# GDN's first half projected from an operand without its norm's factor, gate tiles moved within GDN's order, and the FFN's first tiles kept and interleaved

## The chip, the cores and the metric

The kernel runs on one core of a Trainium2 chip, as one program. The metric is the time of one execution on the device, in microseconds. It is the median of three runs. TensorE is PE below, VectorE is DVE, ScalarE is ACT, GpSimd is POOL; SyncE (SP) issues the transfers (DMAs). Every engine works through its own instructions in program order.

## The reference

It is one inference step of a small decoder trunk: two layers, each a token mixer and a SwiGLU feed forward, on one new sequence of 512 tokens and eight decoding sequences of 4 tokens, 544 tokens of 1024 features in all. The weights are shared.

```python
for i in range(DEPTH):                       # DEPTH = 2
    hn = rms_norm(x, mix_pre_norm[i])
    if i % N_MIXERS == 0:
        out, S, cbuf = gdn_mixer(hn, ...)    # gated DeltaNet
    else:
        out, hs, cbuf = ssd_mixer(hn, ...)   # Mamba-2 SSD
    x = x + rms_norm(out, mix_post_norm[i])
    hn = rms_norm(x, ffn_pre_norm[i])
    f = (silu(hn @ ffn_w_gate[i]) * (hn @ ffn_w_up[i])) @ ffn_w_down[i]
    x = x + rms_norm(f, ffn_post_norm[i])

def rms_norm(x, w):  return x * rsqrt(mean(x * x) + 1e-6) * w

def gdn_mixer(h, ...):                       # 8 heads of 128
    qkv, z, b, a = split(h @ w_in)           # 24 + 8 tiles of 128 columns, and b, a
    q, k, v = split(silu(causal_conv(qkv)))  # 4 taps; then q and k are l2-normed
    beta, g = sigmoid(b), -exp(A_log) * softplus(a + dt_bias)
    o, S = gated_delta_chunked(q, k, v, g, beta, S0)   # a triangular solve per chunk, then a scan
    o = rms_norm(o, norm_w) * silu(z)
    return o @ w_out, S, conv_new
```

Everything is fp32. The outputs are x of all tokens and the new states of both mixers.

## The kernel before, in words

**Layout.** Features lie on the partitions, tokens along the free axis. The 544 tokens are two halves of H2 = 272; half 1 ends with the 32 decoding tokens. Each weight tile of 128 output columns is multiplied with half 0 and with half 1; one such product of a tile with a half is called a *unit*. A unit over 1024 features (8 slices of 128) has 24 matmuls, since an fp32 product is made of three: each operand is split into a high part and a remainder, and `product` (L235) issues wh·xh, wh·xl and wl·xh for each slice (L240 to L242). The b and a columns go through `narrow` (L249).

**Weights.** `fetch_to` loads weights in pieces of 4 slices (256 KB) on SP's queue, AHEAD = 4 pieces ahead of the unit that uses them, into 4 raw buffers. `split` makes wh on ACT (L212) and wl on DVE (L213). A tile whose two units don't follow each other is loaded and split twice.

**Stages.** GDN (b and a, called ba, and 32 tiles k, q, v, z of the eight heads, then wo, its output projection of 8 tiles), FFN0 (22 pairs of a gate tile g and an up tile u, then 8 down tiles of 22 slices, 66 matmuls per unit), SSD (in the same manner; its wo has 16 slices, 48 matmuls per unit) and FFN1.

**Order.** `Flow` carries an estimated clock. Each unit advances it by `flow.product`; the rest of the work (conv, scan, norms) is written as generators, tasks that say with each `yield` after how many estimated microseconds the next step is put into the program. So the delays, constants in the code, set where a step stands among the matmuls of each engine's program; nothing is ordered at run time.

- `start_first(tiles, op, lead)` (L1146) puts `lead` tiles of half 0 first, the same tiles of half 1 next, and takes the rest tile by tile, both halves. GDN has lead 1 (ba alone), FFN0 and FFN1 lead 10 (g and u of five pairs, NL = 5).
- `ab(tiles, op, tail)` (L453) is for the projections at a stage's end: tile by tile, and for the last `tail` tiles all units of half 0 first and then those of half 1. So half 0 is whole `tail` units before the stage ends, and its norm and update run under half 1's units. Tails are 4 in GDN's wo, 3 in the FFN's down and 3 in SSD's wo.

**Norms.** `Squares` squares each feature slice on ACT (L368) and sums on DVE (L375). `rsq` reduces over the partitions with a small matmul (ms, L347), and makes the inverse root of it in a dozen small DVE steps (L319 on). `spread` brings it to all partitions (dg on DVE, L336, then a matmul r, L339). `Pre` is the norm ahead of a stage: with `free=False` each slice is multiplied with the factor (xn, L411) and split into xh and xl, the operand; with `free=True` the operand is made of x times the norm's weight alone (xh L309, xl L310), before the factor is known, and the factor is multiplied to the products. Ahead of both FFNs it is free. `Post` is the norm behind a stage: its `finish` multiplies the projected slices with the factor (fw, L446), adds them to x (L448, every third on POOL) and squares the new x for the next `Pre`.

**GDN's end.** Each head's scan ends with products into `sc` (L978 to L996). A pair's output is normed by `o_norm` (oss L1058, os L1065, then dg, r, a multiply by the weight and factor, L1088, and by silu(z), og, L1091) and split into oh and ol, wo's operand.

Before the first unit, both halves are squared, normed and split, and the flow is drained.

## Time and profile before

| | |
|---|---|
| time, median of 3 runs | 1762.46 us (1761.85 to 1764.05) |
| time of the profiled execution | 1758.35 us |
| its span | 1756.6 us |
| busy: PE, DVE, ACT, POOL | 1680.5, 1165.7, 820.1, 113.0 us |
| mean granted clock of PE | 0.985 |
| GDN with wo | 0 to about 424.6 us |
| FFN0 | to about 849 us |
| SSD with wo | to about 1322 us |
| FFN1 | to 1756.6 us |

Busy time is the time in which an engine executes; matmuls are pipelined, so a busy PE is not yet a PE at full pace. The ends of the stages are read from the first matmul with the next stage's operand. A wait in the profile is the idle time of an engine in front of an instruction, with the instruction that released it.

### The profile page before, as it was taken

Reading aid. Unit: us, or ns where it says so; the run is one execution under the profiler, and the core shown is the slowest. Engines: PE = TensorE matmul, PEld = TensorE weight load, DVE = VectorE, ACT = ScalarE, POOL = GpSimd, SP = SyncE. Lnnn points to the kernel's source line nnn. Section 1 sums busy time; section 2 is a strip of 40 time slices with the busy share of each in tenths; the row PEclk is TensorE's granted clock in tenths of the full one; section 3 lists DMA queues with packets and bytes.
Section 4 is the critical chain, followed back from the end, with each engine's and each line's share of the span. In section 5 each row is a group of like instructions: output and inputs, shape, how many; then the busy total and the mean of one; then the engine's idle time right before and its main releaser. Section 6 shows DMA issues by size and latency. Waiting matters only on the chain. (4 is left out here: it accounts for less than half of the span.)

```text
span 1756.6 us, 37084 instructions
## 1 busy us (share of the span) xinstructions
PE 1680.5 (96%) x14127; PEld 1599.9 (91%) x14127; DVE 1165.7 (66%) x3077; ACT 820.1 (47%) x1830; POOL 113.0 (6%) x335
## 2 busy tenths in 40 slices
PE   4999999998999999999699999999999999999997
PEld 4988888998899999999587899999998999999996
DVE  7895866457876655326878787878358766565346
ACT  4665554445543333325465565657355533333242
POOL 1122112000000000000001110100000000000000
PEclk9999999998999999999899999999999999999998
DMA  5332333343554423225534544432444644444444
GB/s 149 112 90 81 88 91 94 100 140 108 155 176 144 144 98 91 78 82 159 182 110 129 166 142 141 132 105 68 148 134 139 202 141 139 145 141 131 133 142 129
DMA packets 164275, 222.97 MB, mean 127 GB/s; under 512 B 53312, under 2 KB 66176, under 8 KB 163584
## 3 DMA queue, kind: packets, MB, share of 16 engines
q1 hardware_dynamic: 164096, 220.59, 41.5%
q8 instruction: 111, 1.82, 0.4%
q14 instruction: 68, 0.56, 0.1%
HBM read 199.49 MB, written 21.04 MB: 126 GB/s over the span
## 5 line engine op out<-in xcount | busy, mean ns | idle before, releaser
L242 PE MATMUL mm<-xh,wl 128*128 128x272 f32 x2560 | 747.9, 293 | 9.5 <-DVE wl L213 9.1
L240 PE MATMUL mm<-xh,wh 128*128 128x272 f32 x2560 | 752.9, 294 | 0.9 <-ACT raw L533 0.9
L241 PE MATMUL mm<-xl,wh 128*128 128x272 f32 x2560 | 747.2, 292 | 0.0
L212 ACT ACTIVATE wh<-wr 128x512 fp32r<-128x512 f32 (+1 forms) x564 | 349.3, 622 | 415.5 <-PE mm L241 372.3
L213 DVE TENSOR_TENSOR wl<-wr,wh 128x512 fp32r<-128x512 f32 (+1 forms) x564 | 380.3, 678 | 242.0 <-ACT wh L212 230.1
L240 PEld LDWEIGHTS mm<-xh,wh 128*128 128x128 f32 x2560 | 485.6, 190 | 15.6 <-issue 8.6
L242 PEld LDWEIGHTS mm<-xh,wl 128*128 128x128 f32 x2560 | 483.8, 189 | 16.1 <-DVE wl L213 12.2
L241 PEld LDWEIGHTS mm<-xl,wh 128*128 128x128 f32 x2560 | 485.6, 190 | 6.7 <-issue 3.3
L240 PE MATMUL mm<-gb,wh 128*128 128x272 f32 x544 | 157.6, 291 | 0.0
L242 PE MATMUL mm<-gb,wl 128*128 128x272 f32 x544 | 155.3, 288 | 0.0
L241 PE MATMUL mm<-gb,wh 128*128 128x272 f32 x544 | 155.0, 288 | 0.0
L546 DVE SCALAR_TENSOR_TENSOR conv<-raw,cw,conv 128x512 f32<-128x512 f32 x144 | 106.9, 742 | 14.7 <-ACT conv L543 14.0
L240 PEld LDWEIGHTS mm<-gb,wh 128*128 128x128 f32 x544 | 102.2, 188 | 1.3 <-ACT wh L212 0.3
L241 PEld LDWEIGHTS mm<-gb,wh 128*128 128x128 f32 x544 | 102.2, 189 | 0.4
L242 PEld LDWEIGHTS mm<-gb,wl 128*128 128x128 f32 x544 | 101.6, 188 | 0.3
L448 POOL TENSOR_TENSOR x<-x,fw 128x272 f32<-128x272 f32 x16 | 16.1, 1004 | 1069.7 <-DVE fw L446 545.2
L1171 ACT ACTIVATE sg<-sg 128x272 f32<-128x272 f32 x88 | 37.9, 431 | 95.1 <-DVE sg L1170 94.7
L375 DVE TENSOR_TENSOR acc<-acc,sq 128x272 f32<-128x272 f32 x112 | 51.0, 459 | 44.6 <-ACT sq L368 43.9
L241 PE MATMUL mm<-yl,wh 128*128 128x272 f32 x256 | 74.3, 291 | 1.2 <-DVE yl L310 1.2
L242 PE MATMUL mm<-yh,wl 128*128 128x272 f32 x256 | 73.7, 290 | 0.8 <-DVE wl L213 0.8
L240 PE MATMUL mm<-yh,wh 128*128 128x272 f32 x256 | 74.0, 289 | 0.0
L1179 DVE TENSOR_TENSOR sg<-sg,mm 128x272 f32<-128x272 f32 x88 | 38.4, 436 | 50.6 <-PE mm L242 50.3
(398 smaller groups left out, 2456.5 us busy)
## 6 DMA issues: line engine op xcount, KB each, us to landing
wr<-f_d_in SPq DMA_DIRECT2D x110, 256.0 KB
wr<-f_g_in SPq DMA_DIRECT2D x108, 256.0 KB
wr<-f_u_in SPq DMA_DIRECT2D x108, 256.0 KB
wr<-g_w_in SPq DMA_DIRECT2D x64, 256.0 KB
wr<-s_w_in SPq DMA_DIRECT2D x48, 256.0 KB
wr<-s_wo_in SPq DMA_DIRECT2D x44, 256.0 KB
wr<-s_wz_in SPq DMA_DIRECT2D x36, 256.0 KB
ar<-ad SPq DMA_DIRECT2D x32, 272.0 KB
```

The source lines that it names most:

```text
L212: S.activation(out=hi, in_=src, func=AF.Copy)
L213: V.tensor_tensor(out=lo, in0=src, in1=hi.bitcast(F32), op=ALU.subtract)
L240: PE.matmul(ps, lhsT=h[:, k, :], rhs=ah(k0 + k), start=first and k == 0, stop=False)
L241: PE.matmul(ps, lhsT=h[:, k, :], rhs=al(k0 + k), start=False, stop=False)
L242: PE.matmul(ps, lhsT=lo[:, k, :], rhs=ah(k0 + k), start=False, stop=last and k == n - 1)
L375: V.tensor_tensor(out=self.acc, in0=self.acc, in1=self.late, op=ALU.add)
L448: E.tensor_tensor(out=x[:, k, :], in0=x[:, k, :], in1=f, op=ALU.add)
L546: V.scalar_tensor_tensor(out=Y[:, 0:SEQ], in0=R[:, j:j + SEQ], scalar=w[:, j:j + 1], in1=Y[:, 0:SEQ], op0=ALU.mult, op1=ALU.add)
L1171: S.activation(out=t, in_=t, func=AF.Silu)
L1179: V.tensor_tensor(out=t, in0=t, in1=ps, op=ALU.mult)
```

## The change

It has three parts and a number of changed constants.

1. **The first half of GDN without the factor.** `Pre` of half 0 is now free, that of half 1 not (`FREE_G`). Products of half 0 that come before the factor are held in PSUM (`st.held`) and finished when it is there; from then on `scaled` multiplies each product of half 0 with the factor, on DVE, in place of ACT's copy. Both halves' norms are tasks of the flow. Three tiles of half 0 (ba, k0, k1) come first, then the same of half 1 (`GLEAD` = 3). At the head of SP's queue ba's weights and the constants are moved between the halves of x, and the small loads and the zeros are moved behind.
2. **Three gate tiles moved forward.** z0, z1 and z2 stand among the k, q and v tiles; z3 to z7 stay at the end.
3. **Four kept tiles.** g0, u0, g1 and u1 of FFN0 are loaded and split during GDN's wo into buffers of their own (kh, kl). FFN0 starts with them on half 0, then g2.0 g2.1 u2.0 u2.1 … u4.1, then g0.1 u0.1 g1.1 u1.1, then the rest tile by tile (the number behind the dot is the half).

Beside that: the tails are 5 in GDN's wo, 4 in the down projections and 4 in SSD's wo; the delays of the tasks are named constants, some with other values; a sixth buffer for squares, which dg now shares.

```diff
-NSQ = 5
+NSQ = 6
+KEPT = 4
+HELD = 3
-NEWTON = 3.0
+ORDER = ("k0 k1 z0 q0 q1 z1 k2 k3 v0 v1 z2 q2 q3 k4 k5 v2 v3 q4 q5 k6 k7 v4 v5 q6 q7 v6 v7 "
+         "z3 z4 z5 z6 z7")
+GLEAD = 3
+FREE_G = (True, False)
+NEWTON = 2.5
+T_G = 5
+T_F = 4
+T_S = 4
...
@@ emit
+        if len(st.held[0] + st.held[1]) >= (HELD if wide else 2):
+            flow.until(lambda: st.r[hf] is not None)
...
-        done(hf, ps)
+        if st.free[hf] and st.r[hf] is None:
+            st.held[hf].append((done, ps))
+        else:
+            done(hf, ps)
...
@@ Pre.end
+            if self.free:
+                st.ready[self.hf] = True
+                yield 0.0, FACTOR
...
+                while st.held[self.hf]:
+                    done, ps = st.held[self.hf].pop(0)
+                    done(self.hf, ps)
...
+    def scaled(out, ps, hf):
+        if st.free[hf]:
+            V.tensor_tensor(out=out, in0=ps, in1=st.r[hf][0:ps.shape[0]], op=ALU.mult)
+        else:
+            V.tensor_copy(out=out, in_=ps)
...
@@ Conv.done, half 0
+                    if st.free[0]:
+                        scaled(R[:, 3:3 + H2], ps, 0)
+                        ps = R[:, 3:3 + H2]
...
-        order = ("k0 k1 q0 q1 k2 k3 v0 v1 q2 q3 k4 k5 v2 v3 q4 q5 k6 k7 v4 v5 q6 q7 v6 v7 "
-                 "z0 z1 z2 z3 z4 z5 z6 z7").split()
+        order = ORDER.split()
...
-        for u in units(start_first(tiles, xop, 1)):
+        us = units(start_first(tiles, xop, GLEAD))
...
@@ GDN's wo
-        for u in units(ab(tiles, op, tail=4)):
+        todo = [(i, s) for i in range(KEPT) for s in pieces([io["f_u" if i % 2 else "f_g"][0, i // 2]])]
+        us = units(ab(tiles, op, tail=T_G))
+        for n, u in enumerate(us):
             emit(u, True, True)
+            for _ in range(2 - n % 2):
+                if todo:
+                    i, s = todo.pop(0)
+                    kept[i].append(keep(wk, s))
...
@@ ffn
-        for u in units(start_first(tiles, xop, 2 * NL)):
+        if kept is None:
+            us = units(start_first(tiles, xop, 2 * NL))
+        else:
+            first = [[(srcs, hf, xop, done) for srcs, done in tiles[:KEPT]] for hf in range(2)]
+            rest = [(srcs, hf, xop, done) for srcs, done in tiles[KEPT:] for hf in range(2)]
+            n = 2 * (2 * NL - KEPT)
+            us = units(first[0] + rest[:n] + first[1] + rest[n:],
+                       {id(tiles[i][0]): kept[i] for i in range(KEPT)})
```

**The head of SP's queue.** nrm are the norms' weights, cst the constants, wr<-g_ba_in the weights of ba, cw and hist the conv's weights and history, xd<-kqm the zeros. Before:

```order
L103 DMA cst<-cst_in 128x816
L103 DMA nrm<-nrm_in 128x64
L103 DMA x<-xT_in 128x2x272 x8
L103 DMA cw<-g_cw_in 128x96
L103 DMA hist<-g_hist_in 128x576
...
L103 DMA xd_281<-kqm 128x16x16 x2
L103 DMA xd_282<-kqm 128x16x16 x2
L103 DMA wr<-g_ba_in 128x256 x2
L103 DMA wr<-g_w_in 128x512 x2
```

And after:

```order
L133 DMA nrm<-nrm_in 128x64
L133 DMA x<-xT_in 128x2x272 x4
L133 DMA wr<-g_ba_in 128x256
L133 DMA cst<-cst_in 128x816
L133 DMA x<-xT_in 128x2x272 x4
L133 DMA wr<-g_w_in 128x512 x3
L133 DMA cw<-g_cw_in 128x96
L133 DMA hist<-g_hist_in 128x576
...
L133 DMA xd_110<-kqm 128x16x16 x2
```

The weights moved ahead of the small loads and the zeros, and half 1's x behind ba's weights and the constants.

**PE at the end of GDN.** sc are a head's scan products, oss and os the sums of o_norm, mm the wide matmuls: with xh, xl of a z tile, with oh, ol of wo. Before, the last pair's rows stand between matmuls of the z tiles:

```order
L996 MATMUL sc<-E,w 128x128
...
L1058 MATMUL oss<-osq,cst 32x272 x2
...
L1058 MATMUL oss<-osq,cst 32x272 x2
...
L1065 MATMUL os<-cst,oar 68x4 x4
...
L240 MATMUL mm<-oh,wh 128x272
...
L339 MATMUL r<-dg,cst 128x272
```

After:

```order
L1062 MATMUL sc<-w,kp 128x128
L1133 MATMUL oss<-osq,cst 32x272 x2
L279 MATMUL mm<-oh,wh 128x272
L1070 MATMUL sc<-qT,S 128x128
L1071 MATMUL sc<-E,w 128x128
...
L1133 MATMUL oss<-osq,cst 32x272 x2
...
L1140 MATMUL os<-cst,oar 68x4 x4
...
L388 MATMUL r<-dg,cst 128x272 x4
```

The last scan product, the second oss and os moved behind wo's first matmuls; the four spreads r stand together, 37 wide matmuls behind os.

**PE from wo into FFN0.** ms and r are the sum and the spread of a norm; the two xh are the operands of the two halves, kh and kl a kept tile. Before, from half 0's spread on, with half 1's first product at the end:

```order
L339 MATMUL r_6169<-dg_6167,cst_80 128x272
...
L240 MATMUL mm_6405<-xh_6172,wh_6408 128x272
L241 MATMUL mm_6405<-xl_6173,wh_6408 128x272
L347 MATMUL ms_6300<-cst_80,acc_5710 68x1 x4
...
L339 MATMUL r_6369<-dg_6367,cst_80 128x272
...
L240 MATMUL mm_6895<-xh_6372,wh_6824 128x272
```

After:

```order
L388 MATMUL r_6209<-dg_6207,cst_80 128x272
...
L281 MATMUL mm_6350<-oh_5615,wl_6305 128x272
L279 MATMUL mm_6403<-xh_6212,kh_5708 128x272
...
L396 MATMUL ms_6453<-cst_80,acc_5743 68x1 x4
...
L388 MATMUL r_6524<-dg_6522,cst_80 128x272
...
L279 MATMUL mm_6616<-xh_6212,wh_6406 128x272
...
L279 MATMUL mm_6686<-xh_6527,wh_6406 128x272
```

Half 0's spread stands further ahead of FFN0's first matmul, that one uses a kept tile, half 1's sum and spread stand further behind it, and half 1's first product is five units behind, where it was ten.

More of the change, by code (lines that the diff above doesn't have):

```diff
@@ L38 @@
 RAWW = 3 + SEQ + NB * 7
+ORDER = ("k0 k1 z0 q0 q1 z1 k2 k3 v0 v1 z2 q2 q3 k4 k5 v2 v3 q4 q5 k6 k7 v4 v5 q6 q7 v6 v7 "
+         "z3 z4 z5 z6 z7")
+GLEAD = 3
+FREE_G = (True, False)
+FREE_S = (False, False)
+NEWTON = 2.5
+TILE = 1.0
+FACTOR = 5.0
+D_FIN = 2.5
+D_DEC0 = 8.0
+D_DEC1 = 3.5
+D_DEC = 3.5
+D_KT = 3.5
+D_QT = 11.0
+D_VT = 2.5
+D_ON = 3.0
+D_XT = 6.0
+D_WT = 16.0
+D_GT = 2.0
+D_INV = 1.0
+D_MG = 3.0
+D_S1 = 0.8
+D_S2 = 1.2
+D_X3 = 3.0
+D_BT = 1.5
+D_B0 = 0.0
+T_G = 5
+T_F = 4
+T_S = 4
 BIG = 1.0e30
@@ L180, in _program @@
     st.turn = 0
+    st.free = [False, False]
+    st.held = [[], []]
     def half(i):
@@ L233, in fetch_to, with keep, product @@
             ready.append((h, lo))
-    def product(ps, wi, ah, al, first=True, last=True, k0=0):
-        h, lo = ready[wi]
+    def keep(where, src):
+        r = wraw.tile([P, src.shape[1], P], F32, tag="w", name="wr")
+        dma(r, src)
+        h = where.tile([P, src.shape[1], P], F32R, tag="h", name="kh")
+        lo = where.tile([P, src.shape[1], P], F32R, tag="l", name="kl")
+        split(h, lo, r)
+        return h, lo
+    def product(ps, w, ah, al, first=True, last=True, k0=0):
+        h, lo = w
         n = h.shape[1]
@@ L265, in pieces, with units @@
         return out
-    def units(seq):
+    def units(seq, kept={}):
         out, held = [], None
         for srcs, *rest in seq:
+            if id(srcs) in kept:
+                out.append((srcs, *rest, len(plan), kept[id(srcs)]))
+                held = None
+                continue
             if held != id(srcs):
@@ L463, in ab @@
         return seq
-    pres = [Pre(hf, 0, 0) for hf in range(2)]
-    for pre in pres:
-        for k in range(KD):
-            pre.square(k)
-    for pre in pres:
-        flow.start(pre.end())
-    flow.drain()
     from_dram = [io["xT"][:, :, half(0)], io["xT"][:, :, half(1)]]
@@ L638, in ba_done @@
         def ba_done(hf, ps):
-            V.tensor_copy(out=ba[:, half(hf)], in_=ps[0:64])
+            scaled(ba[:, half(hf)], ps[0:64], hf)
             if hf == 0:
@@ L666, in ba_done @@
             rows(gd, Gc)
-            flow.start(decay(0), 8.0)
+            flow.start(decay(0), D_DEC0)
             S.activation(out=neG, in_=Gc, func=AF.Exp)
@@ L704, in k_after @@
                 pr[p].inv = 0
-            flow.start(k_task(h), 4.5)
+            flow.start(k_task(h), D_KT)
         def k_task(h):
@@ L753, in k_task @@
             if pr[p].inv == 2:
-                flow.start(invert(p), 1.0)
+                flow.start(invert(p), D_INV)
         def invert(p):
@@ L807, in invert @@
                 dma(xd[1][p][:, r, r], XT[32 * s:32 * s + 32])
-            flow.start(merge(p), 2.0)
+            flow.start(merge(p), D_MG)
         def merge(p):
@@ L928, in v_after @@
             S.activation(out=v, in_=Y, func=AF.Silu)
-            flow.start(v_task(h, v), 2.5)
+            flow.start(v_task(h, v), D_VT)
         def v_task(h, v):
@@ L965, in ended @@
                 if hasattr(hd[h ^ 1], "ended"):
-                    flow.start(o_norm(p), 3.0)
+                    flow.start(o_norm(p), D_ON)
         def scan(h):
@@ L1112, in gdn, with first @@
             names[id(tiles[-1][0])] = n
-        for u in units(start_first(tiles, xop, 1)):
-            n = names.get(id(u[0]))
-            if n is not None and u[1] == 0 and n[0] == "k":
+        us = units(start_first(tiles, xop, GLEAD))
+        fetch_to(1)
+        dma(cst, io["cst"])
+        load_x(1, 2)
+        fetch_to(3)
+        def first(hf):
+            pre = Pre(hf, 0, 0, FREE_G[hf])
+            for k in range(KD):
+                pre.square(k)
+                yield 0.0, 0.0 if hf == 0 else D_BT
+            yield from pre.end()
+        flow.start(first(0))
+        flow.start(first(1), D_B0)
+        for i, u in enumerate(us):
+            flow.until(lambda: st.ready[u[1]])
+            n = names.get(id(u[0]))
+            if i == 1:
+                load_small()
+            if i == 2 * GLEAD - 1:
+                if GLEAD > 2:
+                    flow.start(decay(1), D_DEC1)
+                load_zeros()
+                og += [act.tile([P, 4, T], F32, tag="x", name="og") for _ in range(2)]
+            if n is not None and u[1] == 0 and i >= GLEAD and n[0] == "k":
                 h = int(n[1])
@@ L1153, in start_first, with ffn @@
         return seq
-    def ffn(layer, last, before, lx, items):
+    def ffn(layer, last, before, lx, items, kept=None):
         fx = ExitStack()
@@ L1225, in ffn @@
             tiles.append(([w], post.tile(m)))
-        for u in units(ab(tiles, op, tail=3)):
+        for u in units(ab(tiles, op, tail=T_F)):
             emit(u, True, True)
@@ L1286, in dt_done @@
             dtT = dt_done.t
-            V.tensor_copy(out=dtT[:, half(hf)], in_=ps[0:64])
+            scaled(dtT[:, half(hf)], ps[0:64], hf)
             if hf == 0:
@@ L1523, in f @@
                     sz[m] = t544("sz")
-                S.activation(out=sz[m][:, half(hf)], in_=ps, func=AF.Silu)
+                t = sz[m][:, half(hf)]
+                if st.free[hf]:
+                    scaled(t, ps, hf)
+                    ps = t
+                S.activation(out=t, in_=ps, func=AF.Silu)
                 if hf:
-                    flow.start(gate(m), 2.0)
+                    flow.start(gate(m), D_GT)
             return f
@@ L1599, in ssd @@
         tiles = [([io["s_wo"][m]], post.tile(m)) for m in range(8)]
-        for u in units(ab(tiles, op, tail=3)):
+        for u in units(ab(tiles, op, tail=T_S)):
             emit(u, True, True)
```

119 lines of the change are left out of this document (70 added, 49 removed).

## The prediction

> **What bounds the kernel.** First the page's busy times, then the chain that ended last, then the waits of PE (us in total, times, longest), to see which engine carries the span and where it stands still.
>
> ```profile
> PE 1680.5 (96%) x14127; PEld 1599.9 (91%) x14127; DVE 1165.7 (66%) x3077; ACT 820.1 (47%) x1830; POOL 113.0 (6%) x335
> PE 23%; DVE 2%; ACT 0%; issue 0%; DVEq 0%; ACTq 0%
> PE ms L347 <- DVE acc L375: 28.2, 6, 11.1
> PE r L339 <- DVE dg L336: 13.6, 5, 6.4
> PE mm L242 <- DVE wl L213: 9.9, 10, 3.1
> ```
>
> PE bounds it: busy 96%, and the chain is PE nearly everywhere. The change takes no matmul away, so it can win only where PE stands still or runs slowly, and the waits say where that is: at the norms (ms waits for the squares' sum, r for the spread factor) and, less, for split weights. The waits name lines, not places, so I cut the span into windows at the seams of the stages (us, busy time and count of PE, PEld, DVE, ACT, POOL, then granted clock, DMA share, GB/s).
>
> ```profile
> 0.00:34.58 34.58, 11.19 (x57) 8.53 (x57) 24.26 (x77) 17.01 (x41) 4.26 (x20) 1.00 0.63 155
> 75.00:125.00 50.00, 48.57 (x646) 43.53 (x644) 46.73 (x171) 31.32 (x83) 12.69 (x42) 1.00 0.41 105
> 314.00:372.30 58.30, 58.30 (x470) 54.86 (x471) 25.97 (x68) 22.61 (x60) 0.66 (x4) 1.00 0.29 90
> 372.30:424.60 52.30, 52.15 (x405) 51.12 (x404) 34.69 (x83) 30.97 (x73) 1.03 (x1) 1.00 0.48 149
> 424.60:475.00 50.40, 41.30 (x295) 39.12 (x294) 44.98 (x128) 28.59 (x62) 3.61 (x3) 0.90 0.41 126
> 475.00:665.00 190.00, 190.00 (x1495) 189.30 (x1494) 124.39 (x275) 69.36 (x133) 0.00 (x0) 1.00 0.44 141
> 832.00:876.00 44.00, 29.31 (x216) 26.57 (x214) 37.91 (x112) 22.60 (x49) 4.34 (x12) 0.87 0.59 190
> 1322.00:1372.00 50.00, 46.65 (x344) 44.90 (x343) 44.76 (x125) 29.00 (x61) 1.75 (x2) 0.93 0.50 154
> ```
>
> The row 475 to 665 is FFN0 in full flow: 1495 matmuls in 190 us, 0.127 us each, nothing idle. A window's loss is its length less 0.127 us for each matmul in it: 12.9 us on the way into FFN0 (424.6 to 475), 16.6 from FFN0 into SSD (832 to 876), 6.3 from SSD into FFN1 (1322 to 1372); wo (372.3 to 424.6) loses 0.9. In the head 57 short matmuls are done in 34.58 us, a loss of about 27. These four places are what the change can reach. In the GDN's interior DVE, 46.7 of 50 us, is nearly as full as PE.
>
> **A, the head: −4 us (bounds −9 and 0).** Columns: start, length, engine, instruction, wait before it in brackets.
>
> ```profile
> 9.76 2.77 ACT L368 ACTIVATE sq<-x 128x272 f32<-128x272 f32 x7
> 10.26 4.73 SPq L103 DMA_DIRECT2D xd<-kqm  x4
> 17.23 1.27 PE L339 MATMUL r<-dg,cst 68*128 68x272 f32 x2 [1.25 <-DVE dg L336]
> 24.95 1.28 PE L339 MATMUL r<-dg,cst 68*128 68x272 f32 x2 [6.44 <-DVE dg L336]
> 25.73 2.31 PE L249 MATMUL mm<-xh,whl 128*64 128x272 f32 x8
> 32.77 0.79 DVE L213 TENSOR_TENSOR xl<-xn,xh 128x272 fp32r<-128x272 f32 x2
> 32.95 1.16 PE L249 MATMUL mm<-xl,whl 128*64 128x272 f32 x8
> 34.58 0.39 PE L240 MATMUL mm<-xh,wh 128*128 128x272 f32 x1
> ```
>
> Before, both halves are squared, normed and split before the first wide matmul at 34.58, half 1's r at 24.95 after a wait of 6.44, and its last xl ends at 33.56. ba and k0, k1 of both halves come after that; four wide units of 24 matmuls, 24 × 0.127 = 3.05 us each, make 12.2, so k1 is done at 34.6 + 12.2 = 46.8. After the change half 0's operand needs no factor: squares and splits run as x lands, and I estimate it complete at 12 us (eight squares and eight copies on ACT, some 0.4 us each, from 5.5 us on). The ba weights are issued before the constants, and the four DMAs of zeros (4.73 us of SP's queue at 10.26) come behind. So ba, k0 and k1 of half 0, two wide units and the narrow ones, are done by about 22, and lie under the making of half 1's operand. Half 1's x now lands behind ba's weights and the constants, so I put its operand 2 us later, at 35.5; with the 1 us of ba behind it, as before, and half 1's own two wide units, 6.1, k1 is done at 42.6. Gain 46.8 − 42.6 = 4. At best half 1, for which ACT and DVE are free sooner, is 3 us earlier than before (−9); at worst its chain slips by the whole gain, since ACT and DVE now also split the first weights there (0). The first x8 of ba takes 2.31 us where the x8 at 32.95 takes 1.16, so PE's start is at half speed; that too now lies under the wait. Half 0's three products are held in PSUM until the factor is there, which nothing on PE waits for before half 1.
>
> **B, the price of the free half: 0 us (−3 to +5).** 33 products of half 0 (24 conv tiles, 8 gates, ba) go through a DVE multiply in place of an ACT copy.
>
> ```profile
> 0.73 1.28 ACT L365 ACT_TABLE_LOAD   x1 [0.73 <-PEq L1695]
> L1179 DVE TENSOR_TENSOR sg<-sg,mm 128x272 f32<-128x272 f32 x88 | 38.4, 436 | 50.6 <-PE mm L242 50.3
> 349.43 0.39 PE L996 MATMUL sc<-E,w 128*128 128x128 f32 x2
> 368.73 0.60 PE L1065 MATMUL os<-cst,oar 128*68 128x4 f32 x8
> 369.37 0.17 DVE L319 TENSOR_SCALAR nx<-os 68x16 f32<-68x16 f32 x1 [2.61 <-PE os L1065]
> 382.70 0.79 DVE L213 TENSOR_TENSOR ol<-og,oh 128x272 fp32r<-128x272 f32 x2 [0.56 <-ACT oh L212]
> L336 DVE TENSOR_TENSOR dg<-cst,ny 68x272 f32<-68x272 f32 x20 | 8.7, 434 | 0.3
> L1091 DVE TENSOR_TENSOR og<-og,qT 128x544 f32<-128x544 f32 x8 | 5.8, 720 | 0.0
> ```
>
> A like multiply out of PSUM takes 436 ns (L1179), so 33 × 0.436 = 14.4 us of DVE over some 330 us, of which eight lie in the quieter gates. Eight xn of about 0.44 go away. ACT is relieved of as much, and gets four more loads of its function table. In the window 75 to 125 PE loses only 1.4 us in all, so there is nothing to win, and DVE's 3.3 us to spare are what covers it; the three gates moved forward bring their units as cover there (their matmuls need little of DVE). The end +5 is four loads of 1.28 us uncovered, the end −3 the 1.4 us of this window and as much again beside it; I take 0, since PE's idle there is so small.
>
> **C, the end of GDN with three gates fewer: +3 us (0 to +27).** Behind the last scan product (349.43) stand, before, 23 us of gates and then wo, all of it PE busy (58.30 of 58.30). The last pair's chain runs beside it: os at 368.73, its norm on DVE, the last ol at 383.49. Six units, 6 × 3.05 = 18.3 us of that cover, move forward. In the new order the last scan product stands behind the first wo matmul, os 21 wide matmuls behind, and from os to the first product with the last pair's operand are 54, 6.9 us. From os on, by row prices: a dozen small DVE steps of 0.17, 2.0; four dg, 1.7; r, 0.6; four multiplies by the factor and two L1091, 3.4; a copy and a subtract, 0.8: 8.5 us, so 1.6 bare, and as much or less at oss and os. By the pace of before, 383.49 − 368.73 = 14.8 us, 7.9 would be bare; the whole chain of before, 34.1, less the 6.9 of cover gives the upper end +27. I take 3, near the row prices, since DVE is 26 of 58 us busy there.
>
> Whether such a stall also costs clock is read from one short idle and one long:
>
> ```profile
> 1324.69 0.39 PE L242 MATMUL mm<-xh,wl 128*128 128x272 f32 x1 [1.94 <-DVE wl L213]
> 1325.38:1332.20 6.82, 6.82 (x43) 6.82 (x42) 4.17 (x21) 1.26 (x2) 0.00 (x0) 0.50 0.37 113
> 864.58:881.64 17.06, 8.27 (x36) 7.24 (x37) 14.36 (x43) 5.56 (x14) 0.76 (x1) 0.50 0.29 97
> ```
>
> Behind an idle of 1.94 us come 6.82 us at a granted clock of 0.50, a loss of half, 3.4 us; on the way into SSD 17.06 us run at 0.50, with PE busy for 8.27 of them. So a bare stall can be paid twice, and my 3 holds half of one drop. [...]
>
> **D, into FFN0: −4 us (−10 to 0).**
>
> ```profile
> 418.11 0.78 DVE L446 TENSOR_TENSOR fw<-fw,r 128x272 f32<-128x272 f32 x2 [0.22 <-PE r L339]
> 431.81 0.49 DVE L310 SCALAR_TENSOR_TENSOR xl<-x,nrm,xh 128x272 fp32r<-128x272 f32 x1
> 436.14 0.44 DVE L446 TENSOR_TENSOR fw<-fw,r 128x272 f32<-128x272 f32 x1 [0.25 <-PE r L339]
> 457.34 0.50 DVE L310 SCALAR_TENSOR_TENSOR xl<-x,nrm,xh 128x272 fp32r<-128x272 f32 x1
> ```
>
> Half 0's update runs from its factor (418.11) to its last xl (432.30), 14.2 us, of which 6.5 lie ahead of wo's end at 424.6. The change does two things here. wo's tail, the units of half 1 behind half 0's last, grows from 4 to 5: 3.05 us more cover, some 9.6 in all. And FFN0's first four tiles (eight pieces, eight DMAs more in wo) are loaded and split during wo, where DVE has 17 us to spare. So half 0's last xl comes some 4.6 us behind FFN0's start; PE needs that slice 2.7 us in, and waits about 2. Against it stands the new order: the first unit of half 1 is the 6th and no longer the 11th, so half 1 is wanted 5 × 3.05 = 15.2 us after the start, before 30.5. Its factor came 11.5 us behind wo's end (436.14) and its last xl 33.2 behind, with nobody waiting. In the new order that factor's matmul stands 9 us behind FFN0's start, 11 with the wait; with the 14.2 us of half 0, half 1 is whole at 25, and PE needs its last slice at 2 + 15.2 + 2.7 = 20. So PE waits 5 to 7 there. Together 9 of the 12.9 us stay: −4. The upper end 0 is half 1 taking back the whole gain; the lower, −10, is half 1's update in the 11 us that its DVE instructions alone would need, and no wait of half 0.
>
> **E, from FFN0 into SSD: −4 us (−6 to 0).**
>
> ```profile
> 848.53 1.31 DVE L411 SCALAR_TENSOR_TENSOR xn<-x,nrm,r 128x272 f32<-128x272 f32 x3 [1.64 <-PE r L339]
> 848.96 0.29 PE L242 MATMUL mm<-gb,wl 128*128 128x272 f32 x1
> 853.52 0.38 ACT L368 ACTIVATE sq<-mm 128x272 f32<-128x272 f32 x1
> 875.65 1.31 DVE L411 SCALAR_TENSOR_TENSOR xn<-x,nrm,r 128x272 f32<-128x272 f32 x3 [1.37 <-PE r L339]
> ```
>
> The last down product ends at 849.25. Half 0's operand starts at 848.53, so its first SSD units trickle along behind it, and half 1's last square, on ACT behind half 0's splits, waits until 853.52; half 1's operand starts at 875.65, 22 us behind. One more down unit in the tail (66 matmuls, 8.4 us) lets half 0's operand, 5 to 6 us of DVE, end ahead of the last product, and that square run 4 us sooner, with half 1's whole chain behind it: −4. What stays is half 1's chain itself, so no more than −6; if DVE merely spreads the same work further, 0.
>
> **G, from SSD into FFN1: −5 us (−7 to 0).** The tail of SSD's wo grows from 3 to 4, units of 48 matmuls, 6.1 us. Half 0's 14 us of update then have 24.4 us of cover where they had 18.3, beside the weights' splits. The whole loss is 6.3 and stems from half 0's operand and one late split (L242 at 1324.69) with the half clock behind it. I take most of it, keep the end −7 for one clock drop less, and 0 if half 1 is late in its place.
>
> The other tails (FFN1's, T_F too) and the steady stages have nothing idle ahead of a seam that I could price: 0. The end of the kernel, 17 us of tail, isn't touched.
>
> **The sum:** −4 + 0 + 3 − 4 − 4 − 5 = −14 us. The profiled run has a span of 1756.6 us and a time of 1758.35, so 1742.6 and 1744.4 in the same execution; the median of the runs is 1762.46, 4.1 above, and 1762.46 − 14 = 1748.5. About 0.2%, 3.5 us, is what a measurement of this kernel can tell from no change.
>
> **Rivals.** R1, the tail of GDN laid bare, slower: the chain at C has 34.1 us from 349.43 to 383.49 and now some 7 of cover. If it needs its pace of before, C is +27 and not +3, and the time 1748.5 + 24 = 1772.5. For it: all steps hang on one another. Against it: before, nobody needed them sooner, and the row prices from os on make 8.5. It decides when C is above 20.5, since the rest is −17. Chance 0.06.
>
> R2, half 1 wanted too soon in FFN0: with an update as slow as the 21.7 us from 436.14 to its last xl, PE waits as long as before and runs at half clock behind it once more, D is +3: 1748.5 + 7 = 1755.5. For it: DVE is busy 45 of 50 us there. Against: several splits of weights stood between. Chance 0.15.
>
> R3, the head gives nothing: if DVE, full in the window from 75 on, is the true bound of the early GDN, a start 4 us sooner only brings PE sooner to DVE's pace, and B's multiplies come on top: 1748.5 + 4 + 2 = 1754.5. For it: 46.7 of 50 us. Against: PE is busy 48.6 in the same 50. Chance 0.12.
>
> R4, the longer tails don't do what they say: half 1's chains start behind the last products as before, and E and G stay: 1748.5 + 9 = 1757.5. For it: E's largest wait is half 1's. Chance 0.10.
>
> R5, more than forecast: A, D and G at their good ends, 1748.5 − 5 − 6 − 2 = 1735.5. Chance 0.07.
>
> **How the numbers follow.** The forecast has 0.42, with 1743 to 1753 as its own range. R2 to R5 alone stay on the fast side; two of R2 to R4 together give 1761 to 1765, within 0.2%, which I put at 0.08. R1's 0.06 ends slower, or within 0.2% where C is less than its end. So faster 0.86, same 0.09, slower 0.05. The range goes from R5's 1735 to 1759, above R4 by what C may add to it.
>
> **What would show it.** A: the first wide matmul at about 16 to 18 us, and the first product behind k1's second half at about 43, where before it was at 47. B: DVE's busy time up by some 10 us and PE's window there as full as before. C: waits of a few us at oss, os or ol behind the last scan product; above 10 us I am wrong there. D: two waits at FFN0's seam, 2 us for half 0 and 5 to 7 for half 1, whose last xl comes about 25 us behind FFN0's start. E: the last square of half 1 within 1 us behind the last down product. G: no half clock behind FFN1's start. The prediction falls if C or half 1 at FFN0 shows more than 15 us of idle PE.

## The result, and the profile after

The changed kernel takes 1748.87 us (median of 10 runs, 1745.21 to 1758.86), the kernel before 1761.04 in the runs beside it. The ratio is 0.9939 with an interval of 0.9918 to 0.9960: faster by 0.6%, 10.7 us by the ratio. The forecast was 1748.5, 14 us below a median of 1762.46. The total came out near the forecast, but two of its terms did not, and their errors cancelled. One execution of all those told of below, of e10, took 3233.59 us and is left out of its ratio, which rests on the other three.

From the changed kernel's page, PE's busy time, and from its waits the first three rows (us in total, times, longest):

```profile
PE 1680.0 (96%) x14127; PEld 1597.6 (92%) x14127; DVE 1177.2 (67%) x3103; ACT 820.0 (47%) x1813; POOL 116.1 (7%) x335
PE ms L396 <- DVE acc L424: 11.9, 5, 8.4
PE r L388 <- DVE dg L385: 10.4, 6, 3.5
PE mm L288 <- DVE whl L243: 8.6, 1, 8.6
```

The waits for ms are 11.9 us where they were 28.2, those for r 10.4 where they were 13.6. The third row is a single wait, that of PE's first products, at 8.62 us, for ba's split weights. PE does the same work. The span is 1745.2 where it was 1756.6, 11.4 less. Not all of that is idle time: PE was busy for 29.9 us at a granted clock of 0.50 before and for 22.4 after, and by an estimate half of the difference, 3.7 us, is clock: in both traces wide matmuls start 0.227 us apart at 0.50 and 0.127 at 1.00 (medians), so taking half, here and below, is a little too much.

Where the time went is best read by counting: both kernels issue the same 11008 matmuls with the operands of projections, in the same number per stage, so the time from the n-th to the m-th is comparable even where their order differs. They are counted from 0: number 1568 is wo's first, 1952 FFN0's. All times are starts in the two traces, the differences taken before rounding.

| stretch (number of the matmul) | before | after | difference | term, forecast |
|---|---|---|---|---|
| start to wo (1568) | 372.3 | 377.3 | +5.0 | A −4, B 0 |
| wo (to 1952) | 52.3 | 54.9 | +2.6 | C +3 |
| into FFN0 (to 2400) | 74.3 | 61.7 | −12.6 | D −4 |
| FFN0 (to 4064) | 213.1 | 213.6 | +0.5 | 0 |
| down (to 5120), into SSD (to 5600) | 137.6 + 111.0 | 139.2 + 107.1 | −2.2 | E −4 |
| SSD (to 7840) | 361.6 | 363.4 | +1.8 | 0 |
| into FFN1 (to 8400) | 83.1 | 76.8 | −6.3 | G −5 |
| FFN1 (to 10400) | 259.1 | 259.1 | 0 | 0 |

The windows of the changed kernel at the same places (length, then busy time and count of PE, PEld, DVE, ACT, POOL, granted clock, DMA share, GB/s):

```profile
0.00:41.15 41.15, 26.36 (x134) 22.98 (x134) 27.69 (x78) 21.55 (x51) 3.96 (x20) 0.88 0.67 178
41.15:377.27 336.12, 324.28 (x3542) 288.31 (x3540) 244.77 (x803) 176.64 (x481) 57.34 (x179) 1.00 0.34 91
377.27:432.20 54.93, 54.08 (x421) 52.23 (x419) 43.87 (x106) 36.79 (x84) 1.89 (x2) 1.00 0.62 200
432.20:475.00 42.80, 42.36 (x331) 40.74 (x330) 37.72 (x114) 20.96 (x48) 2.20 (x3) 1.00 0.24 70
828.00:872.00 44.00, 29.68 (x217) 27.45 (x216) 35.57 (x104) 21.63 (x46) 3.10 (x11) 0.87 0.59 193
1317.16:1361.00 43.84, 43.18 (x347) 42.29 (x346) 40.40 (x106) 27.68 (x57) 1.67 (x2) 1.00 0.57 177
```

And GDN's interior of before, for the second row:

```profile
34.58:372.30 337.72, 334.03 (x3634) 298.40 (x3634) 238.05 (x786) 179.29 (x505) 55.22 (x179) 1.00 0.34 95
```

Into FFN0 PE now stands still for 0.4 us of 42.8, and the clock stays whole; into FFN1 it stands still for 0.7, the clock whole too. In GDN's interior PE now idles 336.1 − 324.3 = 11.8 us where it was 3.7. Into SSD nearly nothing has changed.

**The head.** From the changed kernel's timeline, PE's, ACT's and DVE's rows on half 1's way, with the last of ba's sums at the end:

```profile
20.87 0.72 PE L388 MATMUL r<-dg,cst 68*128 68x272 f32 x2
21.63 0.40 ACT L460 ACTIVATE r<-r 128x272 f32<-128x272 f32 x1 [4.39 <-PE r L388]
26.41 0.65 PE L396 MATMUL ms<-cst,acc 128*68 128x1 f32 x8 [0.57 <-DVE acc L424]
30.57 1.28 PE L388 MATMUL r<-dg,cst 68*128 68x272 f32 x2 [3.50 <-DVE dg L385]
31.88 1.31 DVE L467 SCALAR_TENSOR_TENSOR xn<-x,nrm,r 128x272 f32<-128x272 f32 x3 [1.37 <-PE r L388]
40.99 0.23 PE L720 MATMUL c<-cst,ba 64*32 64x16 f32 x2
```

The same last row in the kernel before:

```profile
36.32 0.23 PE L645 MATMUL c<-cst,ba 64*32 64x16 f32 x2
```

Half 0's r stands on PE behind k0's matmuls; ACT's copy of it waits 4.39 us, and half 1's last four squares stand behind that copy. So half 1's first xn starts at 31.88, and ba's last sums start 4.7 us later than before (40.99 for 36.32). But by then 72 wide matmuls are done, before it was 8: 64 × 0.127 = 8.1 us of work. A is 4.7 − 8.1 = −3.4 us, and B then 5.0 + 3.4 = +8.4. The split depends on the mark: by the forecast's own, the first product behind k1's second half (matmul 128), which starts at 44.27 where before it started at 49.38, A is −5.1 and B +10.1. By either mark B is beyond its range.

**Inside GDN.** Three of PE's waits that the kernel before doesn't have:

```profile
51.24 0.39 PE L279 MATMUL mm<-xh,wh 128*128 128x272 f32 x1 [0.75 <-DVE og L474]
68.53 0.39 PE L279 MATMUL mm<-xh,wh 128*128 128x272 f32 x1 [1.38 <-ACT conv L612]
80.24 0.39 PE L279 MATMUL mm<-xh,wh 128*128 128x272 f32 x1 [2.30 <-ACT og L1175]
```

Each of these units begins only when the product of an earlier one has left its bank of PSUM, 0.75, 1.38 and 2.30 us late. It leaves through DVE's multiply (L474) and, for half 1, ACT; PE waits for both engines' queues, and of these 4.4 us 3.7 end with ACT. Ahead of the last one ACT loads its function table, for a moved gate's silu:

```profile
78.49 1.28 ACT L1175 ACT_TABLE_LOAD   x1
79.79 0.40 ACT L1175 ACTIVATE og<-mm 128x272 f32<-128x272 f32 x1
```

**Into FFN0.** DVE's rows of the changed kernel: half 0's factor used and its last xl, then half 1's.

```profile
422.71 0.79 DVE L509 TENSOR_TENSOR fw<-fw,r 128x272 f32<-128x272 f32 x2 [0.22 <-PE r L388]
436.43 0.50 DVE L359 SCALAR_TENSOR_TENSOR xl<-x,nrm,xh 128x272 fp32r<-128x272 f32 x1
444.20 0.79 DVE L509 TENSOR_TENSOR fw<-fw,r 128x272 f32<-128x272 f32 x2 [0.30 <-PE r L388]
459.76 0.50 DVE L359 SCALAR_TENSOR_TENSOR xl<-x,nrm,xh 128x272 fp32r<-128x272 f32 x1
```

Half 0's update takes 14.2 us as before, 9.5 of them ahead of wo's end at 432.2. Half 1's last xl ends 28.1 us behind wo's end, later than the 25 of the forecast, and still nothing waits.

### The profile page after: what moved, and what is told of

Same layout as the page of the kernel before. It is cut to its first block, busy times and chain, and to the rows that moved or that the text cites. A ratio compares the mean times of both kernels' runs of the same rounds, so it can differ in the third digit from the quotient of the medians.

```text
span 1745.2 us, 37143 instructions
## 1 busy us (share of the span) xinstructions
PE 1680.0 (96%) x14127; PEld 1597.6 (92%) x14127; DVE 1177.2 (67%) x3103; ACT 820.0 (47%) x1813; POOL 116.1 (7%) x335
## 5 line engine op out<-in xcount | busy, mean ns | idle before, releaser
L279 PE MATMUL mm<-xh,wh 128*128 128x272 f32 x2496 | 735.7, 295 | 6.6 <-ACT og L1175 2.3
L280 PE MATMUL mm<-xl,wh 128*128 128x272 f32 x2496 | 727.7, 292 | 0.1
L281 PE MATMUL mm<-xh,wl 128*128 128x272 f32 x2496 | 727.1, 292 | 0.0
L242 ACT ACTIVATE wh<-wr 128x512 fp32r<-128x512 f32 x558 | 345.1, 622 | 408.3 <-PE mm L280 352.6
L243 DVE TENSOR_TENSOR wl<-wr,wh 128x512 fp32r<-128x512 f32 x558 | 376.5, 679 | 222.7 <-ACT wh L242 209.9
L279 PEld LDWEIGHTS mm<-xh,wh 128*128 128x128 f32 x2496 | 473.1, 190 | 23.9 <-issue 9.9
L280 PEld LDWEIGHTS mm<-xl,wh 128*128 128x128 f32 x2496 | 472.9, 190 | 4.7 <-issue 1.2
L281 PEld LDWEIGHTS mm<-xh,wl 128*128 128x128 f32 x2496 | 471.9, 189 | 4.8 <-issue 3.7
L280 PE MATMUL mm<-yl,wh 128*128 128x272 f32 x256 | 74.3, 291 | 1.2 <-DVE yl L359 1.2
```

The costliest lines, as they stand in the source:

```text
L242: S.activation(out=hi, in_=src, func=AF.Copy)
L243: V.tensor_tensor(out=lo, in0=src, in1=hi.bitcast(F32), op=ALU.subtract)
L279: PE.matmul(ps, lhsT=h[:, k, :], rhs=ah(k0 + k), start=first and k == 0, stop=False)
L280: PE.matmul(ps, lhsT=h[:, k, :], rhs=al(k0 + k), start=False, stop=False)
L281: PE.matmul(ps, lhsT=lo[:, k, :], rhs=ah(k0 + k), start=False, stop=last and k == n - 1)
```

## The experiments

Each is the changed kernel with an edit. "wo" is the start of matmul 1568 of the projections, wo's end that of matmul 1952, and the stretches are those of the table above. "ba's sums" are given by the start of their last matmuls. "Half clock" is the time at which the trace's clock records grant 0.50.

**GDN as before (e1_gdn_old).**

```diff
-GLEAD = 3
-FREE_G = (True, False)
+GLEAD = 1
+FREE_G = (False, False)
# and ORDER with z0 to z7 at the end
```

> The changed kernel with GDN's projections as before: no free half, ba alone first, z0 to z7 at the end; kept tiles, FFN0's new order and the longer tails stay. In the changed kernel wo ends at 432.2 us, before at 424.6. Theory F (the free half and the moved gates together cost 7 to 8 us in GDN, more than the head wins): wo ends at about 425, the time is 6 to 8 us below the changed kernel, about -19 against before. Rival S (the 7.6 us come from the longer tail and the kept loads in wo, or from one slow execution): wo ends at 430 or later and the time is within 3 us of the changed kernel.

Ratio 0.9954 (0.9936 to 0.9973), 1750.53 us. wo starts at 384.2 and ends at 437.2. Theory F falls: undoing both, with the new delays and the new head kept, doesn't bring GDN's 424.6 back, so the two edits together aren't the cost. The numbers are those of rival S, but not its reason: wo itself takes 53.0, and the time is lost ahead of it.

**The gates at the end (e2_z_end).**

```diff
# only ORDER, with z0 to z7 at the end
```

> The changed kernel with z0, z1, z2 back at the end; the free half and three tiles first stay. Theory Z (the gates among the other tiles cost PE waits for ACT and DVE, 0.8 and 2.3 us seen at 51 and 80 us, and more in the chain): wo ends 4 to 6 us sooner, at 426 to 428. Theory M (the multiplies on DVE cost it): wo ends within 1.5 us of 432.2. Rival C (the moved gates save idle in the middle): wo ends later than 433.5.

Ratio 1.0020 (1.0001 to 1.0038), 1764.66 us; wo ends at 452.1. Theory Z falls and rival C holds, far beyond its bound: with the free half and the new delays, the moved gates are worth 0.8% of the time, though 27.3 us at half clock ahead of wo are part of it in the profiled execution.

**No free half (e3_no_free).**

```diff
-GLEAD = 3
-FREE_G = (True, False)
+GLEAD = 1
+FREE_G = (False, False)
```

> The changed kernel without the free half and with ba alone first; z0, z1, z2 stay forward. Theory M (the multiplies cost 5 to 8 us, the head wins 2.5): first matmul of k0 at about 34.6, wo ends at 426 to 429. Theory Z: wo ends at 433 to 435, the head's gain lost and nothing won.

Ratio 0.9908 (0.9888 to 0.9928), 1742.79 us. wo starts at 375.9, ends at 435.6. By the end of wo theory M isn't borne out in that execution, in which 6.8 us of wo ran at half clock; 435.6 is nearer theory Z's 433 to 435. The times speak for M: without the free half the kernel is faster than with it, though the two intervals overlap by 0.001. Against the first experiment, whose GDN differs by the gates alone, wo starts 8.3 us sooner, 1.7 of it by clock (e1 has 3.4 us at half clock there): beside the new delays the moved gates are a gain without the free half too.

**One tile first, the half free (e4_lead1).**

```diff
-GLEAD = 3
+GLEAD = 1
```

> The changed kernel with ba alone first, the half stays free. Theory B (with three tiles first ba's second half comes 6 us later than before, and the decays and all heads' chains with it): the waits between 100 and 320 us shrink, wo ends 2 to 4 us sooner, though the head has less to do. Theory M: wo ends at 434 to 436, the head's gain lost and the multiplies still paid.

Ratio 1.0000 (0.9976 to 1.0023), 1757.14 us. ba's sums come at 39.5, hardly sooner, and wo starts at 400.1, of which 47.8 us ran at half clock. Theory B falls: less half of that wo starts at 376.2, the changed kernel by the same count at 372.1. Theory M, that the free half is paid without its head, holds; for wo's end at 456.2 its 434 to 436 allowed nothing for the clock.

**The head as before (e10_oldhead).**

```diff
# beside e3's edit: x of half 1 behind that of half 0 and cst,
# both halves squared, normed and split ahead of the first unit
+        pres = [Pre(hf, 0, 0, FREE_G[hf]) for hf in range(2)]
...
+        for pre in pres:
+            flow.start(pre.end())
+        flow.drain()
```

> No free half, ba alone first, both halves squared and normed ahead of the first unit as before, with half 1's x straight behind half 0's; z0, z1, z2 forward, new delays, kept tiles and longer tails stay. Theory H (in the changed kernels half 1's norm stands on ACT and PE behind half 0's factor and first products, and its operand comes at 40 to 43 us and not at 34): ba's sums end at about 36.5 as before, wo ends 6 to 8 us sooner than in the run without the free half (435.6), at 428 to 430, and the time is about 25 us below before. Rival N (GDN's chains set the time, not its start): wo ends at 434 or later.

Ratio 0.9912 (0.9891 to 0.9933), 1746.94 us. ba's sums come at 37.7, 6.5 us sooner than in e3 (44.2), nearly as theory H has it, but wo starts at 379.4 and ends at 434.2, rival N's figure, with 13.7 us at half clock in GDN. The 6.5 us are not seen in the time. Most of them weren't a gain: matmul 128 starts at 51.0, in e3 at 52.2, since e3 has done 28 wide matmuls more when its sums come. And behind the head 6.8 us ran at half clock; less half of that wo starts at 376.0, in e3 at 375.9. So theory H falls.

**Only the seams (e11_gdn_all_old).**

```diff
# beside e10's edit: ORDER with z0 to z7 at the end, and
-D_KT = 3.5
-D_QT = 11.0
-D_MG = 3.0
-D_S2 = 1.2
-NEWTON = 2.5
+D_KT = 4.5
+D_QT = 9.0
+D_MG = 2.0
+D_S2 = 0.8
+NEWTON = 3.0
```

> The same, and also z0 to z7 at the end and the delays of GDN's tasks and of the norms as before, so that only the kept tiles, FFN0's order and the longer tails differ from before. Theory S (the seams alone bring 12.6 at FFN0, 2 at SSD and 4.7 at FFN1, and GDN's part of the change costs 7.6): wo ends at 424 to 426, the time is 17 to 20 us below before. Rival K (the kept loads and the tail of 5 cost GDN's wo several us): wo ends at 429 or later, the gain is 12 to 14 us.

Ratio 0.9939 (0.9920 to 0.9958), 1750.08 us: as much as the whole change. wo starts at 376.9 with no half clock and takes 56.2, 3.9 more than before, 1.7 of that by 3.4 us at half clock. wo ends at 433.1. So theory S falls and rival K holds by its number, but its reason, the tail of 5 and the kept loads, isn't shown: 2.0 of the 3.9 us are PE's idle, and e1, with the same tail and loads, takes 53.0. The 4.6 us by which wo starts late are lost in the head: ba's sums come 2.3 us later than before, matmul 128 at 53.8 for 49.4. From there to wo are 323.1 us, before 322.9, and e3, with the gates moved and the new delays, takes 323.7: moved gates and new delays together win nothing there. The new delays need the moved gates (e1, with the old order, takes 332.5). Into FFN0 the stretch is 66.8 here and 61.6 or 61.7 with NEWTON at 2.5; 3.4 us at half clock are part of it. NEWTON, the estimate for the norm's small steps, sets where the spread stands in PE's program and is the likely cause of the rest, but other delays went back with it.

**FFN0's order (e5_kept_lead10).**

```diff
+            us = units(start_first(tiles, xop, 2 * NL),
+                       {id(tiles[i][0]): kept[i] for i in range(KEPT)})
```

> The changed kernel with FFN0's first order as before (ten units of half 0, then ten of half 1), its first four tiles still kept for half 0. From the end of wo to matmul 2400 of the wide ones the changed kernel needs 61.7 us where before needed 74.2. Theory O (the gain is half 0's update being hidden, and half 1's late sum and factor no longer stopping the first unit): 60 to 63 us here as well. Rival U (units by turns matter, since half of the splits are saved): 66 us or more.

Into FFN0 62.9 us: theory O. The ten units first cost 1.3 us, no more. The ratio, 0.9958 (0.9931 to 0.9984), hardly differs from the changed kernel's.

**Not kept (e6_order_not_kept).**

```diff
-                if todo:
+                if False:
# no kept pieces; FFN0's order stays
```

> The changed kernel with FFN0's new order, but its first four tiles loaded and split as the others, not kept (loaded again for half 1). From the end of wo to wide matmul 2400 the changed kernel needs 61.7 us. Theory K (the splits between the updates delay half 0): 66 to 72 us. Rival T (the longer tail of wo and the later sums do it): 61 to 64 us.

Into FFN0 70.5 us: theory K. Ratio 0.9975 (0.9957 to 0.9992). PE's longest wait at this seam and its window:

```profile
445.48 0.40 PE L281 MATMUL mm<-xh,wl 128*128 128x272 f32 x1 [3.69 <-DVE wl L243]
441.10:483.90 42.80, 36.98 (x274) 35.01 (x273) 37.96 (x112) 22.13 (x49) 2.14 (x3) 0.96 0.36 113
```

The first tile's wl stands on DVE behind half 0's update, 3.69 us late. The stretch is 8.8 us longer: 5.4 of it is PE's idle (5.8 us in the window, in the changed kernel 0.4), and 3.4 are two drops to half clock, 6.8 us in all, the first of them behind this wait.

**The tails as before (e12_tails3).**

```diff
-T_G = 5
-T_F = 4
-T_S = 4
+T_G = 4
+T_F = 3
+T_S = 3
```

> The changed kernel with the three tails as before (4, 3, 3); GDN and FFN0's order and kept tiles as in the changed kernel. Stretches between wide matmuls of the same number, changed kernel: into FFN0 61.7 us, into SSD 107.2 (before 111.0), into FFN1 76.7 (before 83.1). Theory T (each tail brings its seam's gain): 111 and 83 at the last two, and into FFN0 64 to 66, since the tail covers 3 us of half 0's update. Rival K (kept tiles alone do it there): into FFN0 61 to 63. GDN, which is the same program as in the changed kernel up to wo, shows once more how far one execution differs from another: wo at 370 us plus half of the time at half clock.

Ratio 1.0005 (0.9976 to 1.0033). Into FFN0 69.6 us, and 3.81 us there are one wait at the later spread:

```profile
458.42 0.72 PE L388 MATMUL r<-dg,cst 68*128 68x272 f32 x2 [3.81 <-DVE dg L385]
439.70:481.70 42.00, 35.62 (x262) 34.12 (x261) 35.36 (x109) 18.46 (x44) 3.07 (x3) 0.92 0.20 57
```

Behind it follow 6.8 us at half clock, some 3 us of the loss. Rival K falls: kept tiles and tail are both needed. Into FFN1 81.1, so SSD's tail brings 4.4 us of the 6.3, with no half clock in either execution. At SSD theory T falls: the down stretch is 137.6 and the way into SSD 106.7, together 2.1 less than with the tail of 4; that difference is clock (see E below).

**Half 1's squares first (e14_bt0).**

```diff
-D_BT = 1.5
+D_BT = 0.0
```

> The changed kernel with one delay set to zero: the steps that square half 1 of x are put into the program without 1.5 us between them, so its last four squares stand on ACT ahead of the copy of half 0's factor (which waited 4.39 us for PE at 21.63) and no longer behind it. Theory Q (that place on ACT is what made half 1's operand late): half 1's sum ms before 21 us where it was at 26.4, its first xn before 27 where it was at 31.88, ba's last sums at 35 to 37 where they were at 41, and wo 4 us sooner, if no half clock falls into GDN. Rival P (PE or the transfers hold half 1 back): ba's last sums stay at 39 or later.

Half of theory Q holds. The two rows are half 1's first xn and half 0's spread:

```profile
23.92 1.32 DVE L467 SCALAR_TENSOR_TENSOR xn<-x,nrm,r 128x272 f32<-128x272 f32 x3 [0.22 <-PE r L388]
32.84 1.27 PE L388 MATMUL r<-dg,cst 68*128 68x272 f32 x2 [8.53 <-DVE dg L385]
```

Half 1's xn starts 8 us sooner, but half 0's factor then stands on DVE behind it, PE waits 8.53 us for its spread with half 0's held products in PSUM, and ba's sums come at 44.0, rival P's figure. The place on ACT was a cause of the lateness, not the limit: the two halves' norms share DVE, and one of them is late. Ratio 0.9945 (0.9925 to 0.9966).

**Five tiles first in SSD (e13_slead5).**

```diff
# beside e3's edit
-SLEAD = 3
+SLEAD = 5
```

> The changed kernel without the free half and with ba alone first (0.9908 of before), and with five tiles of half 0 ahead of half 1 in SSD in place of three. The way into SSD still has 13 to 17 us at half clock, in the wait for half 1's operand, 20 us behind the last down product. Theory L (two units more of half 0, 6.1 us, lie in that wait): the stretch into SSD falls from 106 to 100 to 102 us and the time to 5 us below that kernel, about 1737. Rival W (the same units are only done sooner and the wait for half 1 grows by their splits): 104 us or more.

Into SSD 116.4 us, 10 more than in e3, and 5 less behind it: rival W. Of the stretch 27.3 us ran at half clock, in e3 13.7, so the clock is a good part of the 10. Ratio 0.9951 (0.9934 to 0.9968). This seam wasn't won.

**The better version (e15_best).**

```diff
# beside e3's edit
-T_F = 4
+T_F = 3
```

> The changed kernel without the free half, ba alone first, and the tail of FFN's down projections back at 3; the moved gates, the kept tiles, FFN0's order and the tails of 5 and 4 of the mixers stay. Theory N (the tail of 4 there wins nothing: it costs 1.6 us in the down stretch, 139.2 for 137.6, and the way into SSD is 106 to 107 us with either): the down stretch 137.6, into SSD 105 to 108, the time 0.988 to 0.991 of before, 7 us or more below the changed kernel. Rival E (the tail hides half 0's operand): into SSD 109 to 111, the time 0.992 or above.

Ratio 0.9906 (0.9892 to 0.9920), 1742.36 us (1742.03 to 1745.06): 17 us below before, and below the changed kernel's ratio of 0.9939, though the two intervals just touch. The down stretch is 137.6, into SSD 108.6, between theory N's 105 to 108 and rival E's 109 to 111; together they are 246.2, the changed kernel's 246.3. By that sum and by the time it is theory N. Its window of GDN:

```profile
44.00:375.00 331.00, 327.56 (x3581) 293.13 (x3580) 234.96 (x774) 183.40 (x507) 56.37 (x179) 1.00 0.33 93
```

PE idles 3.4 us there, as before the change (3.7), where with the free half it was 11.8.

## Why the prediction was right, and where it was not

**The total** was right because B and D were wrong by 8.4 and 8.6 us in opposite directions, and that is luck. So is the agreement of 1748.87 with 1748.5: the saving is 10.7 us by the ratio where 14 were forecast, and the executions of the changed kernel lie 13.7 us apart.

**A** (−4): measured −3.4. The mechanism holds, half 0's units lie under the making of half 1's operand. The way there was worse than forecast: ba's sums were to be done with k1 at 42.6, and were done at 41.2 with k1's second half still ahead, and from 27.9 on 10.2 us ran at half clock, while I had said that the half clock lies under the wait. The forecast's mark for before, 47, was worked out and not read; it is 49.38 in the trace.

**B** (0, −3 to +5): measured +8.4, beyond the range. The step that failed is "DVE's 3.3 us to spare are what covers it". It compared sums in a window. What matters is when a bank of PSUM is free: the three waits above alone are 4.4 us, and PE's idle in GDN rose by 8.1. The rest stands in the heads' chains, at qk for ACT (1.5) and sk for POOL (1.1) for instance, and which edit moved those steps wasn't isolated. Taking the free half out, with ba alone first, brings that idle from 11.8 to 3.4 (e15). DVE's busy time rose by 11.5 us, as the forecast's sign had it; what it left out is ACT, on which most of the bank waits end. So rival R3 came true in part: B's price came on top and the head's gain was kept, but that DVE is the bound of the early GDN isn't shown. In these executions the price is covered nearly whole: from matmul 128 to wo the changed kernel takes 333.0 us and e3 323.7, but it is at 128 8.0 us sooner. What makes the free half dear is the clock, below. The gates moved forward, put within B at nothing, are a gain only beside the new delays (e1, e2, e11).

**C** (+3): measured +2.6, for another reason. There is hardly a wait in the tail, and none stands in front of these rows:

```profile
377.72 0.39 PE L1071 MATMUL sc<-E,w 128*128 128x128 f32 x2
380.98 0.60 PE L1140 MATMUL os<-cst,oar 128*68 128x4 f32 x8
386.19 2.00 PE L388 MATMUL r<-dg,cst 68*128 68x272 f32 x8
390.46 1.49 DVE L243 TENSOR_TENSOR ol<-og,oh 128x272 fp32r<-128x272 f32 x4
```

From os to the last ol are 391.95 − 380.98 = 11.0 us, where the row prices gave 8.5; the cover was longer too, since the first product with the last pair's operand starts at 389.8 and the last slices are needed later still. Of the 2.6 us, 1.9 are work that moved behind wo's first matmul (16 records of PE more in the stretch), the rest is idle, 0.9 us where it was 0.2. R1 was refuted: the chain's pace of before, 14.8 us from os on, was a pace without need.

**D** (−4, −10 to 0): measured −12.6, nearly the whole loss: PE's idle fell from 9.1 to 0.4 us, and the 10.2 us at half clock that followed the idle before, with PE busy for 7.1 of them, are gone (3.6 by half). Half 0 behaved as forecast, 4.7 us late, and so did half 1, whole 28 us behind. The step that failed is "so PE waits 5 to 7 there". It took PE unit by unit. In PE's program the slices of half 1's first unit stand among those of u2's two units, so the later slices are wanted later: the last of them some 190 matmuls behind FFN0's start, where unit by unit it would be 144. Rival R2, which counts on that wait, falls with it. Two more things in the trace of before were read too lightly: its waits stood at half 1's ms and r inside FFN0's first unit, and these now stand 47 and 72 matmuls behind its start. What carries the 12.6 is told by e5, e6 and e12: without the kept tiles the stretch is 8.8 longer, with the tail of 4 it is 7.9 longer, with the old order of units 1.3. They don't add up to 12.6, and needn't: each was taken out alone, e6 uncovers a wait for wl and e12 one for the spread, and each of the two has 6.8 us at half clock in it.

**E** (−4): measured −2.2. The seam itself won 3.9 us (111.0 to 107.1), as forecast, but the longer tail cost 1.6 in the down stretch, where the forecast had no term. Half 1's last square came 1.5 us behind the last down product, not 4.3, as forecast within 0.5, and half 1's operand 23.0 behind it, not 26.4. The wait for half 1's chain stayed: the first row is that product, the third 8.37 us of PE's idle, the last half 1's operand.

```profile
846.51 0.29 PE L281 MATMUL mm<-gb,wl 128*128 128x272 f32 x1
848.33 0.38 ACT L417 ACTIVATE sq<-mm 128x272 f32<-128x272 f32 x1
865.03 1.04 PE L396 MATMUL ms<-cst,acc 128*68 128x1 f32 x8 [8.37 <-DVE acc L424]
869.85 1.32 DVE L467 SCALAR_TENSOR_TENSOR xn<-x,nrm,r 128x272 f32<-128x272 f32 x3 [1.37 <-PE r L388]
```

With the tail of 3 the two stretches together are 244.3 us (e12) and 246.2 (e15), with 4 they are 246.3 in the changed kernel and 245.3 in e3. Less half of the time for which PE was busy at half clock, they are 241.2 and 241.4 with 3, 241.2 and 241.9 with 4: the tail brings nothing. Before is 242.8 by the same count. What wins the rest against it wasn't isolated; the changed delays are what is left. So rival R4 is right for E; for G, where the tail brings 4.4 us (e12), it isn't.

**G** (−5): measured −6.3, and no half clock behind FFN1's start, as the forecast's sign had it; the 6.8 us of before were 3.4 of the 6.3. That is one execution: e2 to e6, e10 and e13, with the same tail, have 3.4 us at half clock there and take 79 to 80 us. SSD itself took 1.8 us more, which has no term. It is mostly the price of the tail: with 3 (e12) it takes 359.9 us and with 4 360.5 to 361.8 (e3, e4, e10, e11), all with no half clock.

## What to carry to other kernels

Cover isn't a sum over a window: ask at each instruction which buffer it needs back and whose queue returns it. A longer tail has a price in its own stage (1.6 us in FFN0's down projections), to be set against what the seam wins. This kernel, whose stages end in chains, won by moving the late chain's instructions in PE's program (a longer tail, splits done ahead, the sums a few units later): a wait at one instruction held up the matmuls behind it (3.81 us at r in e12, 3.69 at the first wl in e6). Where matmuls with ready and unready operands stand interleaved slice by slice, a late operand may cost next to nothing, as here into FFN0 (0.4 us of PE's idle); read the order, not the units. And take the time at half clock out of a difference before reading a mechanism into it.
